# Six projection chains and the h of two token groups, worked in the order in which the modulation's parts arrive

## The chip, the cores and the metric

The kernel runs on one core of one Trainium2 chip, in one launch. The metric is the device time of that core in microseconds (us). Names of engines: PE is TensorE's matmul, PEld its weight load, DVE is VectorE, ACT ScalarE, POOL GpSimd, SP SyncE, which here only issues DMAs ("SPq" is its queue).

## The reference

Two layers of a diffusion backbone. Nine tiles of 128 tokens go through: eight of the sample, one of the prompt. Layer 0 modulates the normed tokens, projects them, and feeds a convolution branch and an attention branch; layer 1 is a pooling mixer. What the change touches is the start of layer 0:

```python
m = jax.nn.silu(cond) @ w_ada + b_ada             # 1024 -> 3 x 1024, for c and c_ctx
shift, scale, gate = jnp.split(m, 3, axis=-1)
h = rms_norm(x, norm_g) * (1.0 + scale[:, None, :]) + shift[:, None, :]
a, b, ga, q, k, v, gb = jnp.split(h @ w_in, SPLITS_EVEN, axis=-1)
u = a * jax.nn.sigmoid(b)                         # then a depthwise convolution of 31 taps
```

The second modulation (layer 1's, and layer 0's gate) is computed from further columns of `w_ada_0` and from `w_ada_1`.

## The kernel before

Tokens are worked in three groups of 384 (`g` = 0, 1, 2; the prompt's tile is the last of group 2). h is kept transposed, as 8 chunks of 128 channels (`k`) by 384 tokens, split in a high and a low part; weights are split the same way (`split`: a cast on ACT gives `whi`, a subtraction on DVE gives `wlo`). A product is three matmuls per chunk: high with high, high with low, low with high (`chain_ws`, line 232). One unit `c` of the convolution branch takes 256 columns of `w_in_0`, `a` and `b` of 128 channels; for one group it is a pair of chains (`pa_`, `pb_`), 48 matmuls of 384 columns, in two PSUM banks of the tag "mm" (there are four, and two each of "tp" and "cv"). `glu` then frees the banks with a tanh on ACT and a product on DVE.

The first modulation of layer 0 comes in four parts `m`, each four loads of 512 KB (`wada`, line 301); part `m` gives shift and scale of chunks 2m and 2m+1. `ada0(m)` makes its rows on PE (line 312), copies them with DVE (line 318), turns them with one transpose (line 320) and adds the biases. `make_h` transposes three token tiles per chunk on PE (line 419), ACT applies scale and shift (line 424), DVE rounds to the high part, and POOL or DVE makes the low part (line 426). Units c=0 and c=1 run their pairs for group 0 chunk by chunk inside `make_h`. Then the h of group 1 and of group 2 are made, each followed by its pairs.

The other modulation comes in 24 steps (`ada_strips`): each loads a strip of `w_ada` (`wad`) in a slot of the list `ADS` and runs four short matmuls (line 342). These loads are issued after the last x tile's. After its eight steps a strip's rows are copied and turned by `ada_cols`. The convolution's taps run on DVE, and on ACT with POOL, as a stream that `bg` lets on between the pairs. `bias_table` and `bias_windows` fill tables in DRAM (`tbias`, `texp`) for the attention; the first fill is a constant tile `neg` in slot 16.

SBUF is a set of numbered slots. `XS` says in which slot a token tile lies, `WAS` where the loads of the modulation's parts lie. A load can be issued only when its slot's last user is done. Loads on SP are issued one after the other, each waiting for its own conditions. Which instruction of an engine stands where is set by a scheduler ahead of the run, from the order of the code and from costs of its own.

Of the kernel before, what the change touches and what calls it, by code (L numbers as in the profile page):

```python
# [46 lines left out]
def _body(tc, nc, A, O, const, wp, arena, tmpp, smp, psp):  # L47
# [71 lines left out]
    def norm_x(t):  # L119
        if t in normal:  # L120
            return
        normal.add(t)
        if t not in xt:
            load_x(t)
        ss = small(1, "ss")
        se.activation(slot(18, name="junk")[:, :D], xt[t], AF.Square, accum_out=ss)
# [56 lines left out]
    def split(raw, n=WUNIT, c=256):  # L183
# [2 lines left out]
        se.copy(hi[:, :n], raw[:, :n])  # L186
        ve.tensor_tensor(lo[:, :n], raw[:, :n], f(hi[:, :n]), ALU.subtract)  # L187
# [102 lines left out]
    X_AT = {3: (3,)}  # L290
    first_w, wt = {}, {}
    for m in range(4):
        for t in X_AT.get(m, ()):
            norm_x(t)
        for c, u in W0_AT.get(m, ()):
            first_w[c, u] = split(*load_raw0(c, u))
# [9 lines left out]
    def ada0(m):  # L306
        adp = bank("cv")
        for k in range(8):
            for x in range(2):
                for q in range(2):  # L310
                    r = 32 * (2 * x + q)
                    te.matmul(
                        adp[r : r + 2, :P], sc[:, k, :], wt[m, k // 4, x][:, k % 4, q * P : (q + 1) * P],
                        start=(k == 0), stop=(k == 7), tile_position=(0, r),
                    )
        t = ads[m % 2]
        for r in range(0, P, 32):
            ve.tensor_copy(t[r : r + 2, :], adp[r : r + 2, :P])
        adt = bank("cv")
        te.transpose(out=adt[:, :98], in_=t[:98, :], identity=ident[:98, :98])  # L320
        av = adt[:, :P].rearrange("p (x q c) -> p x q c", x=2, q=2)
        fin_shift(0, SH[0], av[:, 0, :, 0:2], 2 * m, 2)
        fin_scale(0, SC[0], av[:, 1, :, 0:2], 2 * m, 2)

    ADS = (12, 13, 14, 15, 16, 17)
    adq = deque()

    def ada_strips(l, col, n, fin):  # L330

        st = {}

        def step(k):
            w = slot(ADS[st_i[0] % len(ADS)], name="wad")[:, : 4 * n]
            st_i[0] += 1
            dma_later(w, A[f"w_ada_{l}"][k * P : (k + 1) * P, col : col + 4 * n])
            if k == 0:
                st["b"] = bank("tp")
            for q in range(4):  # L340
                r = 32 * q
                te.matmul(  # L342
                    st["b"][r : r + 2, :n], sc[:, k, :], w[:, q * n : (q + 1) * n],
                    start=(k == 0), stop=(k == 7), tile_position=(0, r),
                )
# [47 lines left out]

    def ada_rest():
        def fin11(b):
            ada_cols(1, b, 12)
            ada_gate(1, b, G, 1, P)

        ada_strips(0, 2 * D, 256, lambda b: ada_gate(0, b, 256, 0, 0))
        ada_strips(1, 0, G, lambda b: ada_cols(1, b, 0))  # L400
# [8 lines left out]
        return gt  # L409


    def make_h(g, src, l, hs, then=None):

        for k in range(8):
            if then and k % 2 == 0:
                ada0(k // 2)
            b = bank("tp" if k % 2 == 0 or then else "cv")
            for i in range(3):
                te.transpose(out=b[:, i * P : (i + 1) * P], in_=src[i][:, k * P : (k + 1) * P], identity=ident)
            hi, lo = hsl(hs, 0, k, g), hsl(hs, 1, k, g)  # L420
            t = tmp("h")
            for a, e, c in ((0, G, 0),) if g < 2 else ((0, 256, 0), (256, G, 1)):
                s, o = SC[l][:, k, c : c + 1], SH[l][:, k, c : c + 1]
                se.activation(t[:, a:e], b[:, a:e], AF.Identity, bias=o, scale=s)
            ve.tensor_copy(hi, t[:, :G])
            (ve if k % 2 else gp).tensor_tensor(lo, t[:, :G], f(hi), ALU.subtract)
            if then:
                then(k)
# [5 lines left out]

    h0 = {}

    def make_h0(g, then=None):
        for t in range(3 * g, 3 * g + 3):
            norm_x(t)
        h0[g] = hslots(range(4 * g, 4 * g + 4))  # L440
        make_h(g, [xt[t] for t in range(3 * g, 3 * g + 3)], 0, h0, then)


    vs = tc.dram_tile([D, 512], F32, name="vscr")
# [124 lines left out]
    def p_ab(c):  # L569
        def glu(c, g, pa_, pb_):  # L570
# [8 lines left out]
                ve.scalar_tensor_tensor(ut[c][:, d : d + n], th[:, a : a + n], 1.0, pa_[:, a : a + n], ALU.add, ALU.mult)  # L579
            ready[c] = g + 1  # L580

        def fn(W):
            for g in range(3):
                if c == 0 and g == 0:

                    bs = [(units[x], bank("mm"), bank("mm")) for x in range(2)]

                    def then(k):
                        for w, pa_, pb_ in bs:
                            chain_ws(pa_[:, :G], w, 0, h0, g, ks=(k,))  # L590
                            chain_ws(pb_[:, :G], w, P, h0, g, ks=(k,))

                    make_h0(g, then)
                    make_h0(1)
                    late_vectors()
                    for x in range(2):
                        glu(x, g, *bs[x][1:])
                elif c != 1 or g:
                    pa_, pb_ = bank("mm"), bank("mm")
                    chain_ws(pa_[:, :G], W, 0, h0, g)  # L600
                    chain_ws(pb_[:, :G], W, P, h0, g)
                    if c == 0 and g == 1:
                        make_h0(2)
                    glu(c, g, pa_, pb_)
                bg(6000 if c else (0, 0, 0)[g])
                if c or g > 1:
                    ada_steps(2 if c else 1)
# [743 lines left out]
    ada_rest()  # L1351
    streams.append(conv_stream())
    raws = {0: (), 1: ()}
    units = {c: [first_w[c, 0], first_w[c, 1]] for c in range(2)}

    def ensure(i_split, i_raw):
        for j in range(len(items)):
# [43 lines left out]
```

## Time and profile before

| | us |
|---|---|
| median of 3 runs | 982.74 (980.86 to 984.12) |
| the profiled execution | 984.16 |
| its span, first to last instruction | 982.4 |
| PE busy | 950.2 (97%) |
| PEld / DVE / ACT / POOL busy | 864.7 / 602.3 / 404.5 / 367.9 |
| mean granted TensorE clock | 0.991 |

Of the profile's page the chain that ended last is 87% PE and 8% DMA. "Busy" counts a matmul from its start to its modelled end, so overlapping matmuls make a full PE; how much work is done in a stretch is read from the count of matmuls. A number in square brackets after a row of the timeline is the idle time of that engine ahead of it, with what ended it.

### The profile page before, as it was taken

The numbers are of one execution on the slowest core, as the hardware profiler recorded it, in microseconds if no ns is written. First come the engines' busy times: TensorE is split into PE (matmuls) and PEld (weight loads), VectorE is DVE, ScalarE is ACT, GpSimd is POOL, SyncE is SP. The second block draws the span as 40 slices with busy tenths as digits, with TensorE's granted clock in tenths as the row PEclk, the third lists the DMA queues.
The fourth block names the chain that finished last, engine by engine and source line by source line (L and its number), as shares of the span: only waits on it lengthen the run. The fifth ranks groups of instructions, "written<-read, shape, count | busy, mean of one in ns | idle before, by whom it ended". The sixth has DMA issues, their size and how long they took to land.

```text
span 982.4 us, 16659 instructions
## 1 busy us (share of the span) xinstructions
PE 950.2 (97%) x6388; PEld 864.7 (88%) x6388; DVE 602.3 (61%) x1243; ACT 404.5 (41%) x815; POOL 367.9 (37%) x485
## 2 busy tenths in 40 slices
PE   4888999999999999999999999999999999999998
PEld 2786888899999999997777888889999999998887
DVE  3568999999773444447778457556435555575332
ACT  3375666675411244237887323344222222231010
POOL 2264888998843301024456255441000000003322
PEclk9998999999999999999999999999999999999999
DMA  9978653327111111124435412151111111133311
GB/s 300 326 215 277 236 184 133 109 76 244 50 47 46 47 44 43 35 61 137 119 115 176 146 65 108 65 182 43 33 31 35 55 43 54 65 107 115 122 64 66
DMA packets 87531, 108.54 MB, mean 110 GB/s; under 512 B 10700, under 2 KB 73036, under 8 KB 87339
## 3 DMA queue, kind: packets, MB, share of 16 engines
q1 hardware_dynamic: 82539, 95.93, 31.1%
q0 software_dynamic: 2576, 9.18, 2.4%
q10 hardware_dynamic: 2336, 2.36, 0.7%
q8 instruction: 50, 0.82, 0.3%
q14 instruction: 30, 0.25, 0.1%
HBM read 94.64 MB, written 21.57 MB: 118 GB/s over the span
## 4 chain that ended last, share of the span: by engine, by line
PE 87%; DMA 8%; SPq 2%; ACT 1%; DVE 1%; issue 1%; POOL 0%; DVEq 0%; ACTq 0%; POOLq 0%
PE mm L232 37%; PE mm L239 16%; PE mm L1137 10%; PE mm L1130 10%; PE cv L912 3%; PE tp L903 2%; PE mm L879 2%; PE mm L1300 2%; DMA tbias<-in_rpb 2%; PE tp L342 2%; DMA raw<-in_w_out 1%; DMA wada<-in_w_ada 1%; DMA x<-in_x_sample 1%; DMA vwin<-in_cache_v 1%; DMA wad<-in_w_ada 1%; DMA raw<-in_w_in 1%
## 5 line engine op out<-in xcount | busy, mean ns | idle before, releaser
L232 PE MATMUL mm<-h,whi 128*128 128x384 f32 x1536 | 398.3, 339 | 2.9 <-ACT whi L186 1.8
L232 PEld LDWEIGHTS mm<-h,whi 128*128 128x128 f32 x1536 | 277.5, 189 | 10.6 <-ACT gr L474 2.6
L232 PE MATMUL mm<-h,wlo 128*128 128x384 f32 x768 | 258.4, 337 | 0.3 <-DVE wlo L187 0.3
L476 POOL TENSOR_TENSOR zc<-zc,gr 128x384 f32<-128x384 f32 x138 | 150.3, 1090 | 30.9 <-ACT gr L474 21.9
L239 PE MATMUL mm<-whi,h 128*128 128x256 f32 x864 | 157.1, 284 | 0.0
L232 PEld LDWEIGHTS mm<-h,wlo 128*128 128x128 f32 x768 | 145.1, 189 | 1.3 <-issue 0.7
L239 PEld LDWEIGHTS mm<-whi,h 128*128 128x128 f32 x864 | 135.1, 192 | 3.9 <-issue 2.0
L239 PE MATMUL mm<-wlo,h 128*128 128x256 f32 x432 | 122.2, 283 | 0.0
L187 DVE TENSOR_TENSOR wlo<-raw,whi 128x1024 fp32r<-128x1024 f32 (+1 forms) x56 | 69.2, 1236 | 54.1 <-ACT whi L186 53.8
L487 DVE SCALAR_TENSOR_TENSOR cv<-u,convw,cv 128x384 f32<-128x384 f32 (+2 forms) x208 | 95.1, 512 | 0.9
L1137 PE MATMUL mm<-wrh,zs 128*128 128x512 f32 x288 | 92.3, 392 | 1.0 <-POOL wrh L1106 1.0
L1130 PE MATMUL mm<-whi,zs 128*128 128x512 f32 (+1 forms) x304 | 92.4, 379 | 0.0
L186 ACT CAST whi<-raw 128x1024 fp32r<-128x1024 f32 (+1 forms) x56 | 56.9, 1017 | 66.6 <-PE mm L232 23.6
L239 PEld LDWEIGHTS mm<-wlo,h 128*128 128x128 f32 x432 | 82.9, 192 | 0.0
L1144 POOL TENSOR_TENSOR y<-y,og 128x512 f32<-128x512 f32 x34 | 48.5, 1429 | 84.3 <-DVE og L1142 81.2
L474 ACT ACTIVATE gr<-u,convw 128x384 f32<-128x384 f32 (+2 forms) x128 | 64.3, 531 | 30.7 <-POOL zc L476 30.2
L897 POOL TENSOR_SCALAR p<-p,st 128x512 f32<-128x512 f32 x64 | 48.5, 770 | 46.8 <-DVE st L895 30.0
L1130 PEld LDWEIGHTS mm<-whi,zs 128*128 128x128 f32 x304 | 56.0, 188 | 10.6 <-issue 0.2
L1137 PEld LDWEIGHTS mm<-wrh,zs 128*128 128x128 f32 x288 | 53.9, 188 | 12.6 <-POOL wrh L1106 1.4
L1142 DVE TENSOR_TENSOR og<-mm,gr 128x512 f32<-128x512 f32 x34 | 23.3, 688 | 60.3 <-PE mm L1137 35.5
L1130 PE MATMUL mm<-wlo,zs 128*128 128x512 f32 (+1 forms) x152 | 57.2, 378 | 0.0
L456 ACT ACTIVATE th<-mm 128x384 f32<-128x384 f32 x48 | 23.5, 489 | 81.7 <-PE mm L232 81.6
(211 smaller groups left out, 1372.4 us busy)
## 6 DMA issues: line engine op xcount, KB each, us to landing
raw<-in_w_in SPq DMA_DIRECT2D x28, 512.0 KB
wad<-in_w_ada SPq DMA_DIRECT2D x16, 768.0 KB
wada<-in_w_ada SPq DMA_DIRECT2D x16, 512.0 KB
raw<-in_w_in SPq DMA_DIRECT2D x32, 256.0 KB
raw<-in_w_out SPq DMA_DIRECT2D x16, 512.0 KB
y0scr<-y POOLq DMA_DIRECT2D x9, 512.0 KB, 3.2
y<-y0scr SPq DMA_DIRECT2D x9, 512.0 KB
x<-in_x_sample SPq DMA_DIRECT2D x8, 512.0 KB
```

What stands on the lines that cost most here:

```text
L186: se.copy(hi[:, :n], raw[:, :n])
L187: ve.tensor_tensor(lo[:, :n], raw[:, :n], f(hi[:, :n]), ALU.subtract)
L232: te.matmul(out, wsl(units, a, k, c0, P), hsl(hs, b, k, g), start=(k == 0 and i == 0), stop=(k == nk - 1 and i == 2))
L239: te.matmul(out, hsl(hs, p, k, g, a, P), wsl(units, q, k, 0, 256), start=(k == 0 and i == 0), stop=(k == 7 and i == 2))
L474: se.activation(pr[:, o : o + n], src, AF.Copy, scale=w)
L476: gp.tensor_tensor(z, z, pr, ALU.add)
L487: ve.scalar_tensor_tensor(zp if k == 30 else acc, src, convw[:, c, k : k + 1], zp if k == NPTS[c] else acc, ALU.mult, ALU.add)
L897: gp.tensor_scalar(ps[i][:, e, :], ps[i][:, e, :], st[:, 4 + e : 5 + e], 0.0, ALU.mult, ALU.add)
L912: te.matmul(ob[64 * e : 64 * e + 64, i * P : (i + 1) * P], vw[j0 + i][x][:, 64 * e : 64 * e + 64], pts[i][:, e, n * P : (n + 1) * P], star ...
L1130: te.matmul(b[:, c0 : c0 + n], zs[p][:, k, :], WL[k // 2][q][:, k % 2, c0 : c0 + n], start=(k == 0 and i == 0), stop=(k == 7 and i == 2))
L1137: te.matmul(b, zs[p][:, k, :], WR[q][k // 3][:, k % 3, :], start=(k == 0 and i == 0), stop=(k == 7 and i == 2))
L1144: gp.tensor_tensor(yv, yv, t, ALU.add)
```

## The change

The first stretch, up to the end of h of groups 0 and 1, is written out as `first_chains`, whose order on PE, ACT and DVE is kept as written. Three pairs run side by side, (unit 0, group 0), (unit 1, group 0) and (unit 0, group 1); the third uses the two "cv" banks. Each pair of chunks is done for both groups as the modulation's part for it arrives. The tiles x3 to x5 and the first half of unit 1's weights are loaded ahead of part 1; x6, x7 and x8 get other slots (23, 16 and 12). The pair (1, group 1) follows with h of group 2 beside it, then the last two pairs of units 0 and 1; before, unit 1 alone let the taps and the steps on three times, now once. The squares for the norm go to the tile `gr` and not to slot 18. A strip's transposes become a step of their own behind the eight (`ada_turn`), its rows lie in a slot of `ADS` and not in a tile of `tmp`, and `ADS` has another order.

```diff
-    XS = (12, 13, 14, 15, 17, 19, 20, 12, 13)
+    XS = (12, 13, 14, 15, 17, 19, 23, 16, 12)
...
-        se.activation(slot(18, name="junk")[:, :D], xt[t], AF.Square, accum_out=ss)
+        se.activation(gr[:, :D], xt[t], AF.Square, accum_out=ss)
...
+    load_wada(0)
+    raw0[0, 0] = load_raw0(0, 0)
+    raw0[1, 0] = load_raw0(1, 0)
+    for t in range(3, 6):
+        load_x(t)
+    load_wada(1)
+    load_wada(2)
+    raw0[0, 1] = load_raw0(0, 1)
+    raw0[1, 1] = load_raw0(1, 1)
+    load_wada(3)
+    for t in (6, 7):
+        load_x(t)
...
-    ADS = (12, 13, 14, 15, 16, 17)
+    ADS = (14, 15, 17, 13, 16, 12)
...
             if k == 7:
-                fin(st["b"])
+                st["then"] = fin(st["b"])
         for k in range(8):
             adq.append(lambda k=k: step(k))
+        adq.append(lambda: st["then"] and st["then"]())
...
+    def first_chains():
+        bs = {(0, 0): (bank("mm"), bank("mm")), (1, 0): (bank("mm"), bank("mm")), (0, 1): (bank("cv"), bank("cv"))}
...
+        for k in (2, 3):
+            for g in range(2):
+                T(k, g)
+        for m in (2, 3):
+            ada0_rows(m)
+            C(2 * m - 2)
+            ada0_cols(m)
+            T(2 * m, 0)
+            T(2 * m, 1)
+            if m == 2:
+                split_w0(0, 1)
+            C(2 * m - 1, ((0, 0), (1, 0)))
+            T(2 * m + 1, 0)
+            T(2 * m + 1, 1)
+            if m == 2:
+                split_w0(1, 1)
+            C(2 * m - 1, ((0, 1),))
+        for x in bs:
+            for k in (6, 7):
+                C(k, (x,))
...
+            if c == 0:
+                E = mybir.EngineType
+                with tc.manual_schedule(engines={E.PE, E.Activation, E.DVE}):
+                    bs = first_chains()
+                units.update({x: [first_w[x, 0], first_w[x, 1]] for x in range(2)})
+                W = units[0]
+                late_vectors()
+                for x, g in bs:
+                    glu(x, g, *bs[x, g])
+                make_h0(2)
+                chains(1, 1, units[1])
+            for g in range(2 if c < 2 else 0, 3):
+                chains(c, g, W)
+                bg(6000)
+                ada_steps(2 if c else 1)
```

(`C(k, pairs)` runs chunk k's six matmuls of each pair named, `T(k, g)` makes chunk k of h of group g.)

The order on PE around the rows of part 3, before. `mm_255` to `mm_258` are the two pairs of group 0, `wada_239` and the like are part 3's loads, `x_116` is token tile 0, `h_261` is h of group 0 from chunk 4 on.

```order
L232 MATMUL mm_258<-h_259,whi_207 128x384
L232 MATMUL mm_258<-h_260,whi_207 128x384
L232 MATMUL mm_258<-h_259,wlo_208 128x384
L320 MATMUL cv_464<-ident,ads_145 128x98
L312 MATMUL cv_509<-wada_239,sc 2x128 x2
...
L419 MATMUL tp_551<-ident,x_116 128x128
...
L232 MATMUL mm_255<-h_261,whi_200 128x384
```

And now, where `cv_247` and `cv_248` are the pair (0, group 1), `wada_217` to `wada_225` part 3's loads, `x_181` token tile 3 and `h_344` h of group 1:

```order
L443 MATMUL tp_552<-ident,x_116 128x128
...
L443 MATMUL tp_560<-ident,x_181 128x128
...
L230 MATMUL cv_247<-h_344,whi_231 128x384
...
L327 MATMUL tp_578<-wada_217,sc 2x128 x2
...
L327 MATMUL tp_578<-wada_223,sc 2x128 x2
...
L230 MATMUL mm_243<-h_251,whi_536 128x384
...
L338 MATMUL tp_578<-ident,ads_146 128x98
```

Ahead of part 3's rows PE has now done chunks 0 to 3 of three pairs, 72 matmuls; chunk 4 of all three stands behind the rows and ahead of their turning.

ACT at the same place, before: `h_` are the chunks of h as ACT writes them, `x_753` is token tile 6.

```order
L126 ACTIVATE junk_603,ss_602<-x_600 128x1024
L424 ACTIVATE h_555<-tp_551,SH_137,SC_139 128x384
L424 ACTIVATE h_575<-tp_571,SH_137,SC_139 128x384
L424 ACTIVATE h_617<-tp_613,SH_137,SC_139 128x384
L424 ACTIVATE h_625<-cv_621,SH_137,SC_139 128x384
L126 ACTIVATE junk_756,ss_755<-x_753 128x1024
```

And now, with `x_227` token tile 6, `x_229` tile 7 and `x_769` tile 8, `h_641` chunk 6 of group 0:

```order
L186 CAST whi_568<-raw_214 128x1024
L126 ACTIVATE gr_73,ss_757<-x_227 128x1024
L448 ACTIVATE h_641<-tp_637,SH_137,SC_139 128x384
L448 ACTIVATE h_649<-tp_645,SH_137,SC_139 128x384
L126 ACTIVATE gr_73,ss_763<-x_229 128x1024
L448 ACTIVATE h_669<-tp_665,SH_137,SC_139 128x384
L448 ACTIVATE h_677<-tp_673,SH_137,SC_139 128x384
L126 ACTIVATE gr_73,ss_771<-x_769 128x1024
L654 ACTIVATE th_740<-mm_244 128x384
```

The squares of tiles 6 and 7 now stand ahead of chunks 6 and 7 of groups 0 and 1, whose order is kept.

SP's queue from the last token tile on, before. `raw_934` and `raw_937` are the two halves of unit 3's weights, `wad_913` is the first strip's load.

```order
L109 DMA x_771<-in_x_prompt 128x1024
L266 DMA tbias<-neg_940 128x1440
L266 DMA wad_992<-in_w_ada 128x1024
...
L717 DMA tbias<-in_rpb 120x8x16 x2
L266 DMA wad_1069<-in_w_ada 128x1024
L717 DMA tbias<-in_rpb 120x16x16
L717 DMA tbias<-in_rpb 120x8x16 x2
L731 DMA texp<-tbias 384x256 x6
L266 DMA wad_913<-in_w_ada 128x1024
...
L214 DMA raw_934<-in_w_in 128x4x128 x2
...
L214 DMA raw_937<-in_w_in 128x4x128 x2
```

And now, with `wad_994` the first strip's load, `raw_1015` and `raw_1018` unit 3's halves:

```order
L109 DMA x_769<-in_x_prompt 128x1024
L264 DMA wad_994<-in_w_ada 128x1024
...
L264 DMA tbias<-neg_1021 128x1440
L790 DMA tbias<-in_rpb 120x8x16 x2
L264 DMA wad_1214<-in_w_ada 128x1024
L790 DMA tbias<-in_rpb 120x16x16
L790 DMA tbias<-in_rpb 120x8x16
L212 DMA raw_1015<-in_w_in 128x4x128 x2
L264 DMA wad_1291<-in_w_ada 128x1024
L790 DMA tbias<-in_rpb 120x8x16
L212 DMA raw_1018<-in_w_in 128x4x128 x2
L804 DMA texp<-tbias 384x256 x6
```

The first strips' loads moved ahead of the tables; unit 3's halves moved from behind the copies `texp` to between the fills.

More of the change, by code (lines that the diff above doesn't have):

```diff
@@ L289, in _body, with load_wada @@
         norm_x(t)
-    X_AT = {3: (3,)}
     first_w, wt = {}, {}
[L292 to L296, printed above, removed]
+    def load_wada(m):
         for kh in range(2):
@@ L395, in fin11 @@
         def fin11(b):
-            ada_cols(1, b, 12)
+            then = ada_cols(1, b, 12)
             ada_gate(1, b, G, 1, P)
+            return then
         ada_strips(0, 2 * D, 256, lambda b: ada_gate(0, b, 256, 0, 0))
@@ L409, in load_gates, with make_h, h_chunk @@
         return gt
-    def make_h(g, src, l, hs, then=None):
+    def make_h(g, src, l, hs):
         for k in range(8):
[L415 to L428, printed above, removed]
+            h_chunk(g, src, l, hs, k, "tp" if k % 2 == 0 else "cv")
+    def h_chunk(g, src, l, hs, k, tag):
+        b = bank(tag)
+        for i in range(3):
+            te.transpose(out=b[:, i * P : (i + 1) * P], in_=src[i][:, k * P : (k + 1) * P], identity=ident)
+        hi, lo = hsl(hs, 0, k, g), hsl(hs, 1, k, g)
+        t = tmp("h")
+        for a, e, c in ((0, G, 0),) if g < 2 else ((0, 256, 0), (256, G, 1)):
+            s, o = SC[l][:, k, c : c + 1], SH[l][:, k, c : c + 1]
+            se.activation(t[:, a:e], b[:, a:e], AF.Identity, bias=o, scale=s)
+        ve.tensor_copy(hi, t[:, :G])
+        (ve if k % 2 else gp).tensor_tensor(lo, t[:, :G], f(hi), ALU.subtract)
     def hslots(ids):
@@ L435, in _body, with make_h0, C, T @@
     h0 = {}
-    def make_h0(g, then=None):
+    def make_h0(g):
+        h0[g] = hslots(range(4 * g, 4 * g + 4))
         for t in range(3 * g, 3 * g + 3):
             norm_x(t)
-        h0[g] = hslots(range(4 * g, 4 * g + 4))
-        make_h(g, [xt[t] for t in range(3 * g, 3 * g + 3)], 0, h0, then)
+        make_h(g, [xt[t] for t in range(3 * g, 3 * g + 3)], 0, h0)
+    def first_chains():
+        bs = {(0, 0): (bank("mm"), bank("mm")), (1, 0): (bank("mm"), bank("mm")), (0, 1): (bank("cv"), bank("cv"))}
+        def C(k, which=((0, 0), (1, 0), (0, 1))):
+            for x, g in which:
+                w = [first_w[x, 0], first_w.get((x, 1))]
+                for i in range(2):
+                    chain_ws(bs[x, g][i][:, :G], w, i * P, h0, g, ks=(k,))
+        def T(k, g):
+            h_chunk(g, [xt[t] for t in range(3 * g, 3 * g + 3)], 0, h0, k, "tp")
+        h0[0] = hslots(range(4))
+        ada0_rows(0)
+        ada0_cols(0)
+        T(0, 0)
+        T(1, 0)
+        for k in range(2):
+            C(k, ((0, 0),))
+        split_w0(1, 0)
+        for t in range(3, 6):
+            norm_x(t)
+        h0[1] = hslots(range(4, 8))
+        for k in range(2):
+            C(k, ((1, 0),))
+        T(0, 1)
+        T(1, 1)
+        ada0_rows(1)
+        for k in range(2):
+            C(k, ((0, 1),))
+        ada0_cols(1)
+        for k in (2, 3):
[18 more added lines that the diff above has]
+                C(k, (x,))
+        return bs
     vs = tc.dram_tile([D, 512], F32, name="vscr")
@@ L580, in glu, with chains @@
             ready[c] = g + 1
-        def fn(W):
[L583 to L607, printed above, removed]
+        def chains(x, g, W):
+            pa_, pb_ = bank("mm"), bank("mm")
+            chain_ws(pa_[:, :G], W, 0, h0, g)
+            chain_ws(pb_[:, :G], W, P, h0, g)
+            glu(x, g, pa_, pb_)
+        def fn(W):
+            if c == 0:
[13 more added lines that the diff above has]
+                ada_steps(2 if c else 1)
         return fn
@@ L1353, in _body @@
     raws = {0: (), 1: ()}
-    units = {c: [first_w[c, 0], first_w[c, 1]] for c in range(2)}
+    units = {0: None, 1: None}
     def ensure(i_split, i_raw):
```

32 lines of the change are left out of this document (20 added, 12 removed).

## The prediction

> **What bounds the kernel now.** I read the windows of ten microseconds first, to see where TensorE (PE) is not full.
>
> ```profile
> core 0: us, PE busy (x) PEld busy (x) DVE busy (x) ACT busy (x) POOL busy (x), PEclk, DMA share, GB/s
> 0.00:10.00 10.00, 1.00 (x3) 0.47 (x3) 2.07 (x5) 4.95 (x8) 4.09 (x43) 1.00 0.74 257
> 10.00:20.00 10.00, 6.72 (x93) 3.38 (x97) 3.84 (x10) 2.06 (x3) 0.55 (x2) 0.93 1.12 337
> 20.00:30.00 10.00, 7.95 (x73) 5.81 (x66) 5.14 (x9) 2.30 (x3) 1.00 (x1) 0.84 1.14 328
> ...
> 50.00:60.00 10.00, 8.12 (x55) 7.46 (x56) 9.37 (x20) 9.15 (x17) 7.53 (x10) 0.98 0.90 302
> ...
> 80.00:100.00 20.00, 15.32 (x102) 11.49 (x101) 14.28 (x25) 9.19 (x20) 8.73 (x9) 0.83 1.01 332
> 100.00:150.00 50.00, 50.00 (x327) 43.96 (x326) 48.35 (x93) 34.03 (x66) 42.22 (x39) 1.00 0.61 205
> 150.00:200.00 50.00, 50.00 (x384) 43.04 (x383) 49.88 (x120) 34.97 (x70) 45.90 (x45) 1.00 0.35 114
> ```
>
> From 100 us on PE has no gap; before that the DMA share is about 1 and PE starves. What the change can win lies in the first 100 us, and it is won by having more projection matmuls done when PE becomes full. A busy PE hides how few these are, so I counted the matmuls of the projection chains (line 232; 48 make one pair, one unit times one group of 384 columns) in stretches that end at multiples of 48, and took the price of a pair from the chain of waits:
>
> ```profile
> 0.00:44.90 44.90, 12.29 (x52) 9.96 (x52) 0.92 1.03 320
> 44.90:70.05 25.15, 18.01 (x92) 17.01 (x92) 0.93 0.79 244
> 70.05:81.59 11.54, 9.40 (x49) 8.32 (x49) 1.00 0.53 104
> 81.59:98.45 16.86, 9.55 (x49) 8.57 (x48) 0.80 1.05 347
> 98.45:107.95 9.50, 8.60 (x49) 8.28 (x48) 1.00 0.56 198
> ...
> 98.62 0.97 PE tp L342 x16
> ...
> 118.81 8.52 PE mm L232 x48
> ```
>
> A pair costs 8.52 us, 0.178 us a matmul; a step of a strip costs 0.97 / 2 = 0.49 us. So 144 matmuls (25.6 us of work) are done only at 70.05, and the pair from 81.59 to 98.45 takes 16.86 us where the next takes 9.50 with two strip steps. The reasons:
>
> ```profile
> DMA packets 9731, 8.84 MB, mean 340 GB/s; under 512 B 509, under 2 KB 9405, under 8 KB 9729
> ...
> 21.79 0.71 PE L232 MATMUL mm<-h,whi 128*128 128x384 f32 x2
> ...
> 22.75 0.74 PEld L312 LDWEIGHTS cv<-wada,sc 128*2 128x2 f32 x26 [0.17 <-issue]
> 27.80 1.23 DVE L187 TENSOR_TENSOR wlo<-raw,whi 128x1024 fp32r<-128x1024 f32 x1 [1.42 <-ACT whi L186]
> ...
> 43.95 0.75 PEld L312 LDWEIGHTS cv<-wada,sc 128*2 128x2 f32 x28 [0.19 <-DMA wada<-in_w_ada]
> 45.03 1.19 DVE L318 COPY ads<-cv 2x128 f32<-2x128 f32 x4 [1.10 <-PE cv L312]
> 45.43 1.06 ACT L126 ACTIVATE junk<-x 128x1024 f32<-128x1024 f32 x1 [3.81 <-DMA x<-in_x_sample]
> 51.70 0.83 PE L419 MATMUL tp<-ident,x 128*128 128x128 f32 x6
> ...
> 80.75 8.67 DMA wad<-in_w_ada
> 89.55 1.03 PE L342 MATMUL tp<-wad,sc 128*2 128x256 f32 x8 [4.68 <-DMA wad<-in_w_ada]
> ```
>
> The first row is the DMA traffic of 16.04 to 42.04 us. The modulation's last part arrives at 43.95, so chunks 6 and 7 of h cannot exist before, and PE fills that time with two pairs of chains alone. Later it stands 4.68 us at the first strip, whose load sits behind the texp copies, and its clock falls to 0.80.
>
> **The change, step by step.** All against the profiled execution (984.16 us, span 982.4; the median of three runs, 982.74, lies 1.42 lower).
>
> *Arrival.* Ahead of the modulation's last part stand now six x tiles instead of four: 2 x 512 KB more, 1.05 MB / 340 GB/s = 3.1 us. Part 3 is thus read at 47.05 and its rows end at 47.8. This is a loss; part 1, with four more loads of 512 KB ahead (x3 to x5 and a unit's half), comes 2.1 MB / 340 GB/s = 6.2 us later, its last rows near 29 instead of 22.75.
>
> *Work done by then.* PE's new order puts six chunks' worth of chains, for chunks 0 to 3 of three pairs, ahead of part 3's rows: 72 matmuls instead of 48 to 52. They need 72 x 0.178 = 12.8 us between 21.8 (the first chain matmul before; part 0 keeps its place) and 47, with about 4 us of transposes and rows; ACT and DVE, busy 2 to 6 of each 10 us there, cover the rest.
>
> *Tail to 144.* From 47.8: 72 matmuls (12.8 us) and four batches of three transposes. In the x6 row above five starts follow the first within 0.83 less one duration, about 0.11 each: 12 x 0.11 = 1.3 us. ACT has one square ahead of h's chunk 6, x6's: its slot 23 is read by part 3's last rows, so it loads after 47.8 behind some 1.5 MB (4.6 us) queued from 47.05, lands near 53, and the square ends near 54.3. Without it h's chunk 6 could start near 52 (1.19 us of copies, 18 matmuls, 3 small operations). PE has 2.1 us of chunk-5 matmuls to cover that; then the transposes of chunk 7 wait for banks, and x7's square delays chunk 7. I take 2.0 us, between 0 (x6 in time) and 4 (both squares bare, 2 x 1.06, and the 2 us of lateness). Sum: 47.8 + 12.8 + 1.3 + 2.0 = 63.9, against 70.05: **6.1 us won**.
>
> *h of group 2 beside a pair.* 8.52 + 24 x 0.11 = 11.2 against 11.54: 0.3 us.
>
> *The strips.* The strips' first four loads now stand ahead of the bias tables on SP and need only slots that are free once group 0 and 1 are transposed (about 56); the first step comes 230 matmuls in, near 81. No wait: like for like, 16.86 - 8.52 - 3 x 0.49 = **6.9 us won**. The other two steps are done later, at 0.49 each, which changes nothing in the end. Three turns behind the strips move no PE time: no wait on them stands in PE's waits. That the squares go to the gr tile instead of slot 18 I cost at nothing: ACT's order hides it, since nobody reads them.
>
> *What becomes late.* SP's bias fill now waits for x7's slot, since the tile neg is slot 16: for the transposes of group 2, near 74, not 48. And unit c=3's raw weights stand inside that fill:
>
> ```profile
> 40.87 1.30 POOL L709 MEMSET neg<- 128x1440 f32 x1 [4.51 <-PE cv L312]
> 48.58 0.38 SPq L266 DMA_DIRECT2D tbias<-neg  x1
> ...
> 59.43 8.91 DMA tbias<-in_rpb
> 68.42 5.23 DMA tbias<-in_rpb
> 73.67 3.10 DMA tbias<-in_rpb
> ...
> 105.90 1.06 ACT L186 CAST whi<-raw 128x1024 fp32r<-128x1024 f32 x1 [0.34 <-PE mm L232]
> 107.98 1.05 ACT L186 CAST whi<-raw 128x1024 fp32r<-128x1024 f32 x1
> 108.93 0.48 ACT L577 ACTIVATE th<-mm 128x384 f32<-128x384 f32 x1
> ...
> 132.06 0.54 DVE L579 SCALAR_TENSOR_TENSOR u<-th,mm 128x384 f32<-128x384 f32 x1
> ```
>
> neg is set at 74 + 1.3; its table (720 KB) behind one strip load lands near 81 (1.26 MB at 340 GB/s, 3.7 us, and 2 to start). Then come fill 1, fill 3 and the last fill; unit c=3's second half is issued right behind that. If the fills take 3.1 + 5.2 us (nothing beside them) it lands near 95; if 8.9 + 5.2 as before, near 101. In ACT's order the cast of that half stands ahead of the tanh for the pair (1, group 2), whose PSUM banks the second pair after it needs. That pair starts at 63.9 + 11.2 + 9.0 + 9.0 + 9.5 = 102.6, and cast, subtraction, tanh and glu take 1.05 + 1.23 + 0.48 + 0.54 = 3.3 us, so a landing before 99 costs nothing and one at 101 costs 2 us. DVE, full at 49.88 of 50, was already late: the glu at 132.06 comes 4.7 us after its pair ended (118.81 + 8.52). A pause of DVE is passed on. I take 1.9 us, nearer to the contended rows, since strip loads run beside the fills.
>
> Later nothing changes: PE's order is the same row for row from late in the v items to the end, and PE is full there.
>
> **Sum:** 6.1 + 0.3 + 6.9 - 1.9 = 11.4 us. 984.16 - 11.4 = 972.8 for a profiled execution, 971.3 against the median.
>
> **Rivals.**
> (a) *Late raw weights take half of it.* If from neg to the last fill it takes 25.1 us again (48.58 to 73.67), the last half of c=3 lands near 106; the pair at 102.6 then waits 7 us, not 1.9: 13.3 - 7 = 6.3 won, 976.4; with DVE's own loss behind it some 978. For it: the same three fills in a row; against it: in before, six vwin loads and three strip loads ran among them. The Trainium skill's page "DMA: Bandwidth & Descriptors" (anatomy of one DMA) says that DMA engines do not wait on semaphores, the issuing sequencer does; by that rule all behind a waiting fill on SP waits too, and the fences above (59.43, 68.42, 73.67, one after the other) agree.
> (b) *The three pairs don't get ahead.* PE stands before part 1 comes near 29 us and works slowly after each gap:
>
> ```profile
> 29.89 0.84 PE L232 MATMUL mm<-h,whi 128*128 128x384 f32 x2
> ...
> 30.53 0.52 PE L232 MATMUL mm<-h,wlo 128*128 128x384 f32 x1
> ```
>
> From 29.89 to 30.53 two matmuls start and a third follows: 0.32 us each, not 0.178. If 18 of the 72 are left undone at 47.8, 18 x 0.178 = 3.2 us are lost; with some of the tail slow as well, 4.5: 975.8. Against it: the clock is 1.00 in before once work is dense. The Trainium skill's "TensorE: Matmul & The Clock Gate" (Part 1) says that the array starts at half rate and is released after about 3.4 us of sustained work; by it the 24 matmuls after the first gap cost 7.5 us instead of 4.3, still ahead of part 1, and the sum stays. The clock of 0.84 in 20 to 30 us agrees.
> (c) *Slower.* One mechanism, rival (a) carried on: PE's wait for the banks of pair (1, group 2) eats all of 13.3 us if unit c=3's last half lands after 99 + 13.3 = 112, that is 31 us after neg's table landed. At 116 it ends at 986.5. For it: SP does everything in order, and the fill may meet strip loads and texp; against it: 25.1 us was the whole of it before.
> (d) *No change.* The order is made ahead of the run; if x6, part 3 and the raws are all later than I reckon, ACT's order turns each into a stop, and gains and stops cancel, 981 to 985.
>
> **How the numbers follow.** My forecast, 968 to 975, has 0.65; (a) 0.14; (b) 0.09; (c) 0.06; (d) 0.06 in all. 968 is the sum with no c=3 wait and half of the x6 stall; 975 with 5 us lost instead of 1.9. Range 966.5 to 979.5, which takes in (a) and (b). 0.3% is 2.9 us, about what a measurement here can tell: faster 0.88, same 0.05, slower 0.07.
>
> **What would show it.** Right: 144 chain matmuls done near 64 us, 240 near 84, no wait of PE for wad near 80 to 90, and from late in the v items the same rows 11 to 12 us earlier. Wrong: ACT idle before x6's square for over 3 us; PE waiting for DVE u or ACT th near 100; a wait of ACT for raw near 93 to 105; fewer than 65 chain matmuls before part 3's rows. What makes the whole wrong is a wait after 100 us that I hold to be covered, DVE's above all.

## The result and the profile after

The median of six runs is 976.23 us (973.38 to 977.55); the kernel before, timed beside it, has 983.72. The ratio is 0.9920, with a 95% interval of 0.9903 to 0.9937: 7.5 us faster, where 11.4 were forecast. The profiled execution took 977.55 us, the longest of the six; its span is 975.8.

First the windows of the kernel after, for all engines (columns as in the prediction):

```profile
core 0: us, PE busy (x) PEld busy (x) DVE busy (x) ACT busy (x) POOL busy (x), PEclk, DMA share, GB/s
50.00:60.00 10.00, 9.86 (x59) 8.53 (x58) 5.65 (x12) 5.95 (x11) 4.19 (x7) 1.00 0.57 203
80.00:100.00 20.00, 20.00 (x126) 17.72 (x125) 15.38 (x27) 8.72 (x17) 5.51 (x5) 1.00 0.66 139
100.00:150.00 50.00, 50.00 (x326) 44.76 (x324) 48.96 (x105) 35.31 (x71) 43.75 (x41) 1.00 0.71 253
...
170.00:180.00 10.00, 6.85 (x37) 6.67 (x36) 9.88 (x27) 6.74 (x12) 9.29 (x10) 0.66 0.41 133
```

The holes of 50 to 60 and 80 to 100 us are closed. A new one stands at 170 to 180, where PE had none before. The chain matmuls alone (now line 230), in stretches that end at multiples of 48:

```profile
0.00:47.80 47.80, 16.65 (x73) 14.71 (x73) 1.00 1.00 311
47.80:63.36 15.56, 13.46 (x71) 12.30 (x72) 1.00 0.74 267
63.36:74.39 11.03, 10.34 (x50) 8.05 (x50) 1.00 0.14 56
74.39:83.44 9.05, 8.60 (x49) 8.28 (x48) 1.00 0.59 162
83.44:92.50 9.06, 8.59 (x49) 8.27 (x49) 1.00 0.64 107
```

The 144th starts at 63.36 (69.88 before), the 240th at 83.44 (98.28 before). The hole at 170 is the first turn, the transposes of line 390. From PE's timeline and DVE's:

```profile
164.22 0.83 PE L360 MATMUL tp<-wad,sc 128*2 128x384 f32 x8
...
165.32 0.40 PE L237 MATMUL mm<-whi,h 128*128 128x256 f32 x2
...
165.67 0.40 PE L237 MATMUL mm<-whi,h 128*128 128x256 f32 x2
...
174.14 0.72 PE L390 MATMUL tp<-ident,adr 98*128 98x98 f32 x3 [3.15 <-POOL zc L553]
174.56 0.56 PE L237 MATMUL mm<-whi,h 128*128 128x256 f32 x1
...
175.13 0.63 PE L237 MATMUL mm<-whi,h 128*128 128x256 f32 x2
...
175.77 0.63 PE L237 MATMUL mm<-whi,h 128*128 128x256 f32 x2
...
180.00 0.28 PE L237 MATMUL mm<-wlo,h 128*128 128x256 f32 x1
```

```profile
168.85 2.57 DVE L564 SCALAR_TENSOR_TENSOR cv<-u,convw,cv 128x128 f32<-128x128 f32 x6
171.33 0.54 DVE L384 COPY adr<-tp 2x384 f32<-2x384 f32 x1
171.80 0.47 DVE L564 SCALAR_TENSOR_TENSOR cv<-u,convw,cv 128x256 f32<-128x256 f32 x1
172.30 1.70 DVE L384 COPY adr<-tp 2x384 f32<-2x384 f32 x3
```

The strip's last step is at 164.22, PE comes to the turn near 171, and DVE, in the middle of the convolution's taps, ends the four copies at 172.30 + 1.70 = 174.0. The row names POOL, but POOL's own work on that tile, a memset at 147.2, was long done; the copies end just ahead of the start. Behind the wait three matmuls take 175.77 - 175.13 = 0.64 us instead of 0.35, until about 180. That is 3.15 us of wait, and 5.4 us at nearly half rate, in which 5.4 x (1 - 0.35 / 0.64) = 2.4 us are lost: 5.5 us in all.

Before, the same copies stood 0.4 us ahead of PE, which therefore did not wait there. From DVE's timeline of before, and then PE's:

```profile
162.93 1.70 DVE L364 COPY adr<-tp 2x384 f32<-2x384 f32 x3
```

```profile
165.02 0.42 PE L367 MATMUL tp<-ident,adr 98*128 98x98 f32 x3
```

How far the two sides of the turn had come can be counted. PE's 576 matmuls of the chains and DVE's taps of the convolution up to the 116th before (this window also takes in the start of the 117th), then the same two after, each in a window from zero (the first number behind the window's length is the busy time, with the count beside it):

```profile
0.00:167.40 167.40, 109.64 (x576) 101.76 (x576) 0.95 0.76 241
```

```profile
0.00:159.40 159.40, 57.79 (x117) 0.95 0.79 248
```

```profile
0.00:150.00 150.00, 109.29 (x576) 101.28 (x576) 1.00 0.75 242
```

```profile
0.00:152.30 152.30, 56.30 (x116) 1.00 0.75 239
```

PE was 17.4 us ahead. Of that some 4.4 us are strip steps put off (by then PE had spent 12.26 us on them before, 7.89 after), so 13 us are true gain. The taps on DVE were only 7.1 us ahead (6.9 by the starts of the 116th), and 7.5 us is what the kernel won. This reading was a theory at that point: the turn ties PE to the convolution's stream, and what PE gains beyond the stream is lost there. The length of the wait does not follow from the two gains alone, since the turn itself has moved: PE comes to it near 171 instead of 165, and DVE's copies stand behind 29 taps more than before.

### The profile page after: what moved, and what is told of

It reads as the page before. It is cut to its first block, busy times and chain, and to the rows that moved or that the text cites. A ratio compares the mean times of both kernels' runs of the same rounds, so it can differ in the third digit from the quotient of the medians.

```text
span 975.8 us, 16659 instructions
## 1 busy us (share of the span) xinstructions
PE 948.4 (97%) x6388; PEld 866.3 (89%) x6388; DVE 601.9 (62%) x1243; ACT 404.4 (41%) x815; POOL 369.8 (38%) x485
## 4 chain that ended last, share of the span: by engine, by line
PE 82%; POOL 5%; DVE 3%; DMA 3%; ACT 2%; issue 2%; SPq 1%; DVEq 0%; ACTq 0%; POOLq 0%
PE mm L230 33%; PE mm L237 15%; PE mm L1210 10%; PE mm L1203 10%; POOL zc L553 5%; PE cv L985 3%; PE tp L976 2%; PE mm L952 2%; PE mm L1373 2%; DVE cv L564 1%; DMA x<-in_x_sample 1%; DMA raw<-in_w_in 1%; PE tp L443 1%; SPq L212 1%; PE cv L230 1%
## 5 line engine op out<-in xcount | busy, mean ns | idle before, releaser
L230 PE MATMUL mm<-h,whi 128*128 128x384 f32 x1504 | 389.5, 339 | 1.0 <-POOL h L450 0.4
L230 PEld LDWEIGHTS mm<-h,whi 128*128 128x128 f32 x1504 | 271.6, 189 | 6.8 <-issue 2.0
L230 PE MATMUL mm<-h,wlo 128*128 128x384 f32 x752 | 252.8, 337 | 0.0
L237 PE MATMUL mm<-whi,h 128*128 128x256 f32 x864 | 160.6, 287 | 0.0
L237 PEld LDWEIGHTS mm<-whi,h 128*128 128x128 f32 x864 | 137.4, 194 | 6.5 <-ACT vst L694 3.3
L230 PEld LDWEIGHTS mm<-h,wlo 128*128 128x128 f32 x752 | 141.9, 189 | 0.0
L564 DVE SCALAR_TENSOR_TENSOR cv<-u,convw,cv 128x384 f32<-128x384 f32 (+1 forms) x208 | 95.8, 514 | 1.3
```

Of the source, the lines that this page charges most:

```text
L230: te.matmul(out, wsl(units, a, k, c0, P), hsl(hs, b, k, g), start=(k == 0 and i == 0), stop=(k == nk - 1 and i == 2))
L237: te.matmul(out, hsl(hs, p, k, g, a, P), wsl(units, q, k, 0, 256), start=(k == 0 and i == 0), stop=(k == 7 and i == 2))
L564: ve.scalar_tensor_tensor(zp if k == 30 else acc, src, convw[:, c, k : k + 1], zp if k == NPTS[c] else acc, ALU.mult, ALU.add)
```

## The experiments

All ran beside the kernel before, with four to six executions each; its median was 984.39, 984.08 and 983.82 us in the three groups of four. In the table, the marks are the start of the nth chain matmul, and the start of the one behind the nth matmul of the v items that follow the chains (256 columns, 1296 of them). They are counted in each trace, that is in one execution, which need not be the median one.

| kernel | median us | ratio, 95% interval | chains 144 | 240 | 576 | v 108 | v 162 | v 1242 |
|---|---|---|---|---|---|---|---|---|
| before | 983.72 | 1 | 69.88 | 98.28 | 167.30 | 183.9 | 191.3 | 323.2 |
| after | 976.23 | 0.9920 (0.9903-0.9937) | 63.36 | 83.44 | 149.92 | 166.5 | 178.5 | 316.3 |
| e1 | 971.52 | 0.9879 (0.9866-0.9893) | 63.74 | 83.82 | 150.30 | 166.9 | 174.5 | 311.6 |
| e2 | 974.05 | 0.9899 (0.9882-0.9917) | 63.65 | 83.72 | 148.60 | 165.2 | 172.6 | 316.1 |
| e3 | 974.43 | 0.9907 (0.9893-0.9922) | 64.18 | 84.26 | 151.39 | 172.2 | 179.7 | 315.2 |
| e4 | 979.64 | 0.9954 (0.9942-0.9967) | 69.80 | 94.06 | 163.08 | 179.7 | 187.1 | 318.8 |
| e5 | 972.57 | 0.9878 (0.9864-0.9891) | 63.37 | 83.45 | 149.93 | 166.5 | 175.2 | 312.3 |
| e6 | 974.41 | 0.9899 (0.9886-0.9913) | 62.44 | 82.55 | 149.03 | 165.6 | 176.4 | 313.5 |
| e7 | 978.39 | 0.9938 (0.9924-0.9951) | 63.13 | 82.48 | 148.97 | 165.6 | 180.9 | 318.3 |
| e8 | 972.95 | 0.9882 (0.9869-0.9896) | 63.19 | 83.27 | 149.10 | 165.7 | 173.1 | 311.3 |
| e9 | 976.96 | 0.9926 (0.9913-0.9938) | 63.49 | 82.85 | 155.77 | 172.4 | 179.1 | 316.2 |
| e10 | 980.92 | 0.9968 (0.9955-0.9980) | 63.53 | 82.89 | 151.25 | 167.8 | 182.1 | 319.5 |
| e11 | 972.20 | 0.9883 (0.9869-0.9896) | 63.18 | 83.26 | 149.09 | 165.7 | 173.1 | 309.9 |
| e12 | 969.57 | 0.9857 (0.9842-0.9872) | 62.24 | 82.36 | 148.19 | 164.8 | 172.2 | 309.0 |

### The turn (e1, e2, e3, e8)

e1, the turn's copies on ACT:

```diff
-            ve.tensor_copy(t[r : r + 2, :], b[r : r + 2, :G])
+            se.copy(t[r : r + 2, :], b[r : r + 2, :G])
```

> The changed kernel with the four copies of a turn put on ACT instead of DVE; nothing else differs in PE's order up to the second turn. Theory 'late copies': in the changed kernel PE stands 3.15 us at the turn's transposes (174.14) because DVE, full, ends the copies only at 173.99, and its clock is 0.66 in 170 to 180 us; ACT comes to the copies some 5 places earlier, right behind the second v item's copy, near 168. Then there is no PE wait at the turn, 54 of the v items' matmuls take about 7.4 us there as elsewhere instead of 12.0, and the median falls by 4 to 5 us, to 971 to 972.5. Rival 'five more steps and late glus': the time lost between the chains and the v items' end is strip steps and DVE's general lateness, the turn's wait only shows it; then the median stays at 975 to 977.5.

971.52 us, as the theory of late copies had it. From the timeline of ACT and then of PE, and the windows, in its trace:

```profile
170.49 1.44 ACT L384 COPY adr<-tp 2x384 f32<-2x384 f32 x3
```

```profile
172.07 0.45 PE L390 MATMUL tp<-ident,adr 98*128 98x98 f32 x3 [0.70 <-ACT adr L384]
```

```profile
170.00:180.00 10.00, 9.30 (x79) 8.34 (x78) 10.00 (x29) 7.20 (x14) 7.92 (x9) 1.00 0.41 133
```

The wait is 0.70 us and the clock stays at 1.00. The chains are not earlier than in the changed kernel (150.30 at 576, against 149.92); the stretch from v 108 to v 162 takes 7.6 us instead of 12.0, and the end is 4.7 us earlier. The two ratios' intervals do not meet. So the turn cost the changed kernel 4 to 5 us.

e2, each turn two units later:

```diff
+        adq.append(lambda: None)
+        adq.append(lambda: None)
         adq.append(lambda: st["then"] and st["then"]())
```

> The changed kernel with each turn two more units behind its strip (three instead of one). PE's transposes of the first turn move 168 rows later (about 23 us), DVE's copies 25 rows later (about 15 us), so the copies should lead by some 5 us instead of following by 3. Theory 'late copies': no PE wait at the turn, no dip of the clock there, 971 to 973. Rival 'five more steps and late glus': 975 to 977.5. Third possibility, the wait only moves: DVE slips as much as PE does, a PE wait of 1 to 3 us stands at the new place, 974 to 976.

The third possibility came: the first turn no longer waits, but the second does, where the queue of steps is emptied at the first q/k item and nothing is left to put ahead of it. PE's timeline, of the execution that took 976.79 us (three of the six took 972.16 to 972.96, at a mean clock of 1.000):

```profile
222.04 0.72 PE L392 MATMUL tp<-ident,adr 98*128 98x98 f32 x3 [3.33 <-DVE adr L386]
```

e3, the turn at once behind its strip:

```diff
+                if st["then"]:
+                    st["then"]()
...
-        adq.append(lambda: st["then"] and st["then"]())
```

> The changed kernel with the turn done at once behind its strip, as before the change (the part 'a unit behind' undone; the copies' tile still takes a slot of the strips' ring). DVE's copies stand 14 rows earlier than in the changed kernel, PE's transposes 52 rows earlier (about 7 us). Theory 'late copies': copies and transposes both come about 7 us earlier, so a wait of 0 to 3 us, median 971.5 to 976; it tells whether putting the turn behind brought the wait. If putting it behind helps by itself: slower than the changed kernel, 977 to 981, with a longer PE wait at the turn.

974.43, no slower than with the turn behind; the wait is there too, earlier and shorter:

```profile
167.53 0.45 PE L391 MATMUL tp<-ident,adr 98*128 98x98 f32 x3 [2.25 <-DVE adr L385]
```

So putting the turn behind did not bring the wait, nor did it help: at once or one unit behind, DVE ends its copies 2 to 3 us after PE has come to the transposes.

e8, e1 with the turns one unit later (e2's edit with one empty step):

> The first experiment's kernel with the turns one more unit behind their strips (two instead of one). There PE still stands 0.7 us at 172.0 for ACT's copies. Theory 'late copies': the transposes move 72 rows (10 us), the copies on ACT 6 places: wait gone at both turns, 970.5 to 971.5, and all runs close together. Rival: ACT slips with PE, or the second turn waits: 971.5 to 974.

972.95, not better than e1: its first turn does not wait, but the second stands 1.17 us at 217.97 for ACT's copies. This is e2's result in small.

### Where the strips' gain comes from (e4, e5, e9, e10)

e4, the kernel before with the strips' slots of the change:

```diff
-    ADS = (12, 13, 14, 15, 16, 17)
+    ADS = (14, 15, 17, 13, 16, 12)
```

> The kernel before with one line changed: the strips' slots in the order 14, 15, 17, 13, 16, 12, so the first three strip loads need only slots that are free once groups 0 and 1 are transposed, and stand ahead of the bias tables and of texp on SP. Theory (the prediction's strips term): PE's 4.68 us wait at 89.55 and the clock of 0.80 behind it go, 6.9 us won alone: 976 to 978. Rival 'hidden anyway': the pair at 81.59 is slow because the DMA queues are full and DVE is late, the strip's wait is replaced by another; then 980 to 984. If the term holds, the new order of the first pairs brings the other 6 us and something takes 5 back; if not, the change's whole gain is the pairs'.

The wait for wad is gone from PE's waits, the clock is 1.00 from 80 to 100 us, and 4.75 us are won, not 6.9: a result between the two ranges. From the 144th to the 288th chain matmul it takes 33.76 us against 37.90 before, both with five strip steps: 4.1 us. The first steps now stand in small pieces among the pair at h of group 2, which takes 15.20 us (11.54 before).

e5, e1 with the old slots (the reverse of e4's edit):

> The changed kernel with the turn's copies on ACT (the first experiment's kernel, 971.5 us) and the strips' slots back in the old order 12, 13, 14, 15, 16, 17. In SP's order the first strip's load then stands behind three later strip loads and six vwin loads, but still one place ahead of neg's table. Theory A, the slots' order brings the strips' gain: the wait for wad comes back, +4.7 to +6.9 us, 976 to 978.5. Theory B, the gain comes from the tables, which now wait for the slot of x7 and so stand behind the strips whatever the strips' slots are: the first load needs slot 12 (x8, transposed near 74 us) and lands near 77 to 79, its step stands near 81, no wait: 971 to 973.

972.57: in the changed kernel the slots' order is worth nothing that shows (Theory B). What stands ahead of the strips is not decided by it alone, so e9 and e10 put the tables early again, with either order of the slots:

```diff
-        t = slot(16, name="neg")
+        t = slot(20, name="neg")
```

> The first experiment's kernel with both candidates for the strips' gain undone: the strips' slots in the old order, and neg in slot 20, which is free early as slot 16 was before the change, so its table, the fills and two texp copies stand ahead of the first strip's load on SP again. Theory B of the fifth experiment (the gain comes from tables that stand behind the strips): PE waits 3 to 6 us for wad near 81 to 90 us, clock under 0.9 there, 976 to 978.5. Rival: the first strip needs its rows at 81 and the tables, with the DMA queues less full by then, are through by 78: 971 to 973.

> The first experiment's kernel with neg in slot 20 alone (the tables early again, the strips' slots as in the change). The first strip's load then stands one place ahead of neg's table, three more ahead of the fills. If either of the two (new slots, late tables) is enough for the strips' gain: no wait for wad, 971 to 973. If only late tables bring it: a wait of 3 to 6 us, 976 to 978.5.

e9 is 976.96 and has the old wait again. Its PE timeline, and its chain matmuls from the 192nd to the 240th and on to the 288th:

```profile
87.32 1.03 PE L360 MATMUL tp<-wad,sc 128*2 128x256 f32 x8 [4.14 <-DMA wad<-in_w_ada]
```

```profile
74.52:82.85 8.33, 8.33 (x50) 8.33 (x49) 1.00 0.37 77
82.85:98.35 15.50, 10.40 (x50) 10.08 (x49) 0.78 1.06 334
```

These two pairs, with one step in them, take 23.83 us (the trace lists each of a step's four matmuls as two). In the changed kernel they take 18.11 with the same one step (74.39 to 92.50, above; it begins in the first of the two there). The wait and the clock behind it thus cost 5.7 us, where the prediction had 6.9; in the medians e9 lies 5.4 us behind e1, by the ratios 4.6.

e10 missed both expectations: no wait for wad, as with new slots, but 980.92, the slowest of all. Its SP queue and PE timeline:

```profile
84.83 6.45 SPq L804 DMA_DIRECT2D texp<-tbias  x7
91.38 2.19 SPq L212 DMA_DIRECT2D raw<-in_w_in  x2
```

```profile
104.57 0.62 PE L230 MATMUL mm<-h,whi 128*128 128x384 f32 x2 [1.81 <-ACT th L654]
...
177.70 0.72 PE L390 MATMUL tp<-ident,adr 98*128 98x98 f32 x3 [5.38 <-ACT adr L384]
```

The table's texp copies now stand ahead of all of unit c=3's raw weights, whose first half is issued at 91.38. In the changed kernel that half is out at 87.66, and texp comes behind both:

```profile
87.66 1.10 SPq L212 DMA_DIRECT2D raw<-in_w_in  x2
...
91.54 3.20 SPq L212 DMA_DIRECT2D raw<-in_w_in  x2
97.31 3.83 SPq L804 DMA_DIRECT2D texp<-tbias  x6
```

So in e10 the weights of c=3 are late, DVE stands 8.1 us for them (3.4 in e1), the tanh of a pair is late, PE waits 1.81 us, and the turn, one more time, takes the larger part: its wait is 5.38 us, in e1 0.70. The four cases in a row: tables late 971.5 and 972.6, tables early 977.0 and 980.9. Against the wait for wad either is enough, late tables (e5) or the new order of `ADS` (e10, and e4 in the kernel before); it comes back only without both (e9). But tables that stand early hold up the weights of c=3 instead, and only their going behind, which x7 in slot 16 does, avoids that too.

### The other terms (e6, e7)

e6, e1 with the squares of x6 and x7 behind h on ACT:

```diff
         for x in bs:
             for k in (6, 7):
                 C(k, (x,))
+        for t in (6, 7):
+            norm_x(t)
         return bs
```

> The first experiment's kernel with the squares of x6 and x7 pinned behind the last chunks of h on ACT (norm_x(6) and norm_x(7) written at the end of first_chains). The prediction costs these squares ahead of h's chunks 6 and 7 at 2.0 us. If that is right, 144 chain matmuls are done near 61.7 to 62.5 us instead of 63.7 and the median falls to 969.5 to 970.5. Rival: the chunks wait for part 3's rows, banks and DVE anyway, and x6 and x7 come later for h of group 2, which then is late: 144 at 63 to 64, 971 to 973.

Half of the expectation held. The 144th chain matmul starts at 62.44 instead of 63.74, and PE keeps 1.3 us up to the 576th. The median is slower, 974.41. PE's timeline and a window:

```profile
172.58 0.72 PE L390 MATMUL tp<-ident,adr 98*128 98x98 f32 x3 [2.49 <-ACT adr L384]
```

```profile
170.00:180.00 10.00, 7.51 (x52) 7.40 (x51) 10.00 (x31) 7.38 (x14) 8.30 (x9) 0.83 0.42 136
```

PE came to the turn earlier, ACT did not. It waited 1.8 us longer than in e1, and the clock fell as well: an earlier PE ended later. The edit did not leave the stream alone, though. DVE's 116th tap starts at 152.29 instead of 151.35, so the longer wait is an earlier PE and a later stream together. The intervals of e6 and e1 overlap at their ends (0.9886 and 0.9893); every execution of e6, from 973.60 us on, is slower than every one of e1, up to 973.31.

e7, e1 with `bias_table()` at i == 3 instead of i == 1:

> The first experiment's kernel with the bias table written two units later (i == 3 instead of 1): the raw weights of unit c=3 then stand ahead of neg's table and the fills on SP, so they land some 10 us earlier. The prediction charges their lateness 1.9 us. If that is right: 969 to 970. If it costs nothing, because PE never reaches the pair that needs the banks before the glu is done: 971 to 972, the marks of the chains the same within 0.3 us. If the tables' later fills now meet other loads: 972 to 974.

978.39, outside all three. Up to the 576th matmul its marks differ from e1's only by 0.6 us at 144 and by the first matmuls of a strip step, which stand behind the 240th (0.7 us); from 240 to 576 it takes 66.49 us, e1 66.48. So the late raw weights cost PE's chains nothing in e1. They did cost DVE's stream something. First the changed kernel on DVE's timeline, then e7, where the same twelve taps come 4.5 us earlier without a wait for ACT's `whi` (in e1 they start at 101.03):

```profile
96.41 1.23 DVE L187 TENSOR_TENSOR wlo<-raw,whi 128x1024 fp32r<-128x1024 f32 x1 [3.59 <-ACT whi L186]
...
99.64 1.22 DVE L187 TENSOR_TENSOR wlo<-raw,whi 128x1024 fp32r<-128x1024 f32 x1 [0.95 <-ACT whi L186]
...
101.84 6.39 DVE L564 SCALAR_TENSOR_TENSOR cv<-u,convw,cv 128x384 f32<-128x384 f32 x12
```

```profile
97.31 6.39 DVE L564 SCALAR_TENSOR_TENSOR cv<-u,convw,cv 128x384 f32<-128x384 f32 x12
```

What went wrong is another transfer that fell behind the tables. In DVE's waits from 80 to 150 us, and on PE's timeline:

```profile
DVE gr L412 <- DMA gb<-in_b_ada: 8.8, 1, 8.8
```

```profile
176.51 0.72 PE L390 MATMUL tp<-ident,adr 98*128 98x98 f32 x3 [6.47 <-ACT adr L384]
```

DVE stood 8.8 us for a bias row, PE noticed nothing until the turn, and there it waited 6.47 us. This is the strongest test of the tie, though it was not meant as one. Less the 3.7 us that it had been ahead of e1, the stream is some 5 us late (the 116th tap starts at 156.71, in e1 at 151.35); PE's chains are on time, the turn waits 5.8 us longer than in e1, and the kernel is 6 to 7 us slower (5.8 by the ratios, 6.9 by the medians).

### Away from the tie (e11, e12)

e11, copies on ACT, the first turn one unit later, the second left for the next unit:

```diff
             if pr == 0:
-                ada_steps()
+                ada_steps(len(adq) - 1)
+            if pr == 1:
+                ada_steps()
```

> The copies on ACT, the first turn two units behind its strip, and the second turn left for the start of the next projection unit (its queue of steps is emptied but for the last, and that one is done a unit later). Theory 'the turn ties PE to the convolution's stream on DVE and ACT': no PE wait at either turn, clock 1.00 from 100 to 300 us, 970 to 971. Rival, something else late in the v items or the q/k items stops PE as soon as the turns don't: 971.5 to 973.

No wait for adr of 0.5 us or more is left in PE's waits and the clock is 1.00 from 100 to 300 us, but 972.20 is no better than e1, whose own 0.70 us hardly cost anything (of the profiled executions e11's is 1.6 us the faster, of the medians e1's is 0.7). The rival's time came, without the stop that it spoke of.

e12, e11 and e6 together:

> The eleventh kernel with the squares of x6 and x7 behind the last chunks of h as well. In the sixth experiment this put PE 1.3 us ahead at 576 chain matmuls (149.03 against 150.30) and the turn's wait took all of it. If the tie to the stream is what took it: 1.3 us less than the eleventh kernel, 968.7 to 969.8. If PE meets the stream elsewhere (banks of the glu, the v items' copies): as the eleventh, 970 to 971.

969.57, in the range that the tie gave. The windows of e12:

```profile
150.00:200.00 50.00, 50.00 (x419) 45.30 (x420) 47.68 (x104) 36.76 (x73) 44.75 (x41) 1.00 0.60 201
200.00:250.00 50.00, 50.00 (x428) 47.13 (x427) 43.45 (x79) 30.51 (x56) 45.19 (x44) 1.00 0.40 133
```

The same edit that cost e1 2 to 3 us (e6) gains e11 2.6, once the turns no longer tie PE to the stream. In the marks it is 0.9 us all the way to v 1242. From that mark to the end of the span every trace of the table takes 658.3 to 659.9 us (before 659.2, after 659.5), so what the change and the experiments do shows ahead of it; e12's 658.3 against e11's 659.7 gives most of the rest, and is no more than the traces differ there. e12 beats both kernels: ratio 0.9857 (0.9842 to 0.9872), 14 us under before.

## Why the prediction was right, and where it failed

The sign, the size of the first hundred microseconds and the range held; 7.5 us are two thirds of the 11.4 forecast. Of the signs named for a right forecast, 144 near 64 us, 240 near 84 and no wait for wad came; the rows late in the v items came 6.9 us earlier (v 1242), not 11 to 12. Two of the signs named for a wrong one came as well: ACT idle for over 3 us before x6's square (5.68), and ACT waiting for raw (4.51). Point by point:

- *Arrival.* Part 3's rows were to end at 47.8: they start at 45.93 and take 1.93, as said. But no wait stands ahead of them: PE came straight from the chains, so it was PE's order and no longer the arrival that set the moment, and that both fall together is luck.
- *Work done by then.* 72 were forecast, and 72 stand ahead of the rows (the 73rd starts at 47.79). Rival (b) did not happen, although PE was as slow as it said at first, 0.32 us a matmul until 26.3. Its sum for the first 24 matmuls, 7.5 us, is not what 3.4 us at half rate add to 4.3; 7.5 is what they took all the same (20.23 to 27.71, a gap of 0.4 us included).
- *Tail to 144.* 63.9 forecast for the end of the 144th, which starts at 63.36 and ends near 63.7. The 2.0 us for the squares were a little large: e6 frees 1.3, e12 0.9. ACT's row is the one forecast (near 53, the square late for x6):

```profile
52.58 1.06 ACT L126 ACTIVATE gr<-x 128x1024 f32<-128x1024 f32 x1 [5.68 <-DMA x<-in_x_sample]
```

- *h of group 2 beside a pair.* 11.2 forecast, 11.03 measured.
- *The strips.* No wait for wad, as forecast; e9 prices it at 5.7 us where 6.9 stood. The reason, the strips' new slots, is one of two, and either is enough: the loads stand ahead of the tables with the old slots too, because the tables moved (e5), and the new slots alone do it as well (e10). The prediction counted the moved tables only as a cost.
- *Late raw weights of c=3: 1.9 us forecast as a wait for PSUM banks, nothing measured there.* ACT did wait for them, and the cast began at 95.33:

```profile
95.33 1.05 ACT L186 CAST whi<-raw 128x1024 fp32r<-128x1024 f32 x1 [4.51 <-DMA raw<-in_w_in]
98.55 1.06 ACT L186 CAST whi<-raw 128x1024 fp32r<-128x1024 f32 x1 [0.79 <-DMA raw<-in_w_in]
```

  The second half thus landed near 98.5, between the 95 and the 101 of the prediction and within the 99 that it held to be free; it took the later end. e10 shows the price beyond the limit: 1.81 us at once. But the lateness was not free: DVE stood 3.59 and 0.95 us behind that cast, and had no time later to make it up (48.96 us busy in 100 to 150). The copies that PE waits for at the turn are 3.15 us late, so without these 4.5 us they would have come in time. This is argued from e7's and e10's rows above; no run has these weights early and nothing else late.
- *The step that failed: "Three turns behind the strips move no PE time: no wait on them stands in PE's waits."* It cost 5.5 us in the profiled execution and 4 to 5 in the medians (e1). That no wait stood there before was true. The copies stood there with 0.4 us to spare, and the change brought PE 13 us forward and DVE's taps 7.1. The sentence "A pause of DVE is passed on" was in the prediction, and "DVE's above all" among what would make it wrong; neither was worked out at the one place after 100 us where PE's order contains something that DVE must finish first.

With the two terms put right the sum closes: 11.4 + 1.9 - 5.5 = 7.8, against 7.5 measured. This books the losses by the place where PE lost them; the 5.5 at the turn very likely holds the lateness of c=3's weights. Without the turn's wait and without the c=3 term the prediction's own terms give 13.3; e1 gave 984.39 - 971.52 = 12.9 (11.9 by the ratio).

Rival (a) would have given 976.4, almost the measured time, by raw weights that land near 106. They landed near 98.5, and the wait that it put at the pair's banks did not occur: from 240 to 576 PE kept its pace. If the reading above holds, it had the cause right in part, by another way, DVE's stream and the turn. A time that fits is no evidence for the rival that named it.

## What to carry to other kernels

When a change moves one engine forward, look through its order for every place where it takes something from an engine that does not move forward as much, and write down how much time is in hand there; an absent wait says only that it is not negative. A transfer that comes late without stopping the bound engine can still hold up the slower stream, and come out at the next such place. Make the sum for the slower stream as well as for the bound engine. Where a small job for the bound engine must pass through a full engine, give it to another one or leave room behind it, at both ends of the queue.

## What the runs showed of the hardware

Short waits of PE cost more than their length, from a certain length on. With 0.70 us (e1) and 1.70 us (e5) of wait at the turn the clock in 170 to 180 us stayed at 1.00; with 2.49 (e6) it was 0.83, with 3.15 (after) 0.66, and with 2.25 (e3) 0.83 in the ten microseconds from 165. These are means. Windows of 3.4 us show that the clock was either full or half: half from 168.5 to 171.9 in e3, from 172.2 to 175.6 in e6, and for two such stretches in after. The windows of after, and then e5's with its wait:

```profile
169.70:173.10 3.40, 1.29 (x11) 1.08 (x10) 3.36 (x9) 2.35 (x5) 3.10 (x4) 1.00 0.25 81
173.10:176.50 3.40, 2.36 (x12) 2.39 (x13) 3.35 (x8) 2.47 (x5) 3.15 (x4) 0.50 0.22 45
176.50:179.90 3.40, 3.40 (x18) 3.40 (x18) 3.37 (x13) 1.99 (x4) 3.17 (x4) 0.50 0.74 267
```

```profile
169.60:173.00 3.40, 1.70 (x16) 1.52 (x14) 3.40 (x9) 3.29 (x7) 2.03 (x3) 1.00 0.24 81
```

In after PE stood for 2.1 us of the first window, and the clock halved at its end, while PE was still waiting. The last 1.0 us of the wait fell in the next window, and the clock came back only behind the one after that, in which PE was busy throughout. In e5 1.7 us without work in a window left the clock full. The Trainium skill's "TensorE: Matmul & The Clock Gate" (Part 1) has the array at half rate after an idle window of about 3.4 us and released after as long a busy one. The half rate (0.64 us for three matmuls against 0.35) and the busy window before the release agree; the idle one was not needed in full here, 2.1 us of it were enough. In the runs of the changed kernel the wait sits near this edge, which fits its spread: 973.38 to 977.55, with mean clocks of 0.999 to 0.996, where e12's four runs lie between 969.20 and 969.83.
